# Dense-block gates of a two-layer PEER kernel: one block per layer placed by indirect scatter-add instead of matmul

## The chip, the cores and the metric

The kernel runs on one core of one Trainium2 chip, as one launch. The metric is the device time of one execution in microseconds (us), here the median of three runs. TensorE is called PE (its weight loads PEld), VectorE DVE, ScalarE ACT, GpSimd POOL and SyncE SP. SP issues the plain transfers, POOL the indirect ones; a queue means one engine's instructions, which it takes strictly in the order in which they were compiled.

## The reference

Two layers (DEPTH = 2) work on a latent stream of 512 tokens and a context stream of 256, all of width 1024, in float32. Each layer is a token mixer (a gated recurrence and a short convolution, not touched by the change) and a PEER channel mixer, cut here to what matters:

```python
def peer_ffn(h, wq, subkeys, u, v):
    scores = einsum('bthpd,hpkd->bthpk', (h @ wq)..., subkeys)
    s1, i1 = top_k(scores[..., 0, :], 16)
    s2, i2 = top_k(scores[..., 1, :], 16)
    cand = s1[..., :, None] + s2[..., None, :]
    top, pos = top_k(cand, 16)
    eidx = take_along_axis(i1 * 128 + i2, pos)
    gate = softmax(top)
    act = gelu(einsum('ted,td->te', u[eidx], h))
    return einsum('te,ted->td', gate * act, v[eidx])
```

Every token has 8 heads with 16 experts each out of 128 x 128 = 16,384. A gate is the softmax weight of one (token, expert) pair; an expert that two heads of a token choose gets the sum of both gates.

## The kernel before, in words

The 768 tokens are six blocks of 128: blocks 0 and 1 are the context, 2 to 5 the latents. A layer runs `mixer` and then `peer`. In `peer`, some blocks are **gathered**: for each of the 128 picks of a token, one indirect transfer on POOL (L875) brings 128 rows of 4 KB of U into a tile `gr` or `gs`, DVE multiplies and sums it (L882), and after a gelu the same is done with V (L891). The others are **dense**: all 16,384 experts are computed and multiplied by a gate matrix that is zero where an expert was not picked. In layer 0 blocks 0 and 1 are gathered and 2 to 5 dense (`nt` = 512 tokens). In layer 1 block 5 is gathered, 2 to 4 are dense but for the last 32 tokens of block 4 (`REST`), which are gathered (`nt` = 352).

`peer` goes through four stages:

- **Scores.** `proj` with `wq`, then `top16` and `top_pairs` on DVE.
- **Gates.** `pick` prepares the indices of the first gathered block, and its U gathers start. Then, for each dense block, `select` works out i1, i2 and the gates, and `gates` (L754) turns them into the gate matrix. Per token this is one 128 x 128 float32 matmul of two one-hot matrices (L789, PE); DVE and ACT build the one-hot matrices oA and oB (L773 to L784), ACT copies the result into `stg` (L790), and SP writes 32 tokens at a time, 2 MB, to the DRAM tensor `gd` (L791). Between them, `ahead` computes some of the U products of the dense stage (`experts_in`, a pair of key rows at a time: 48 matmuls, L306 to L308) and writes them to the DRAM tensor `ad`. `AHEAD` = (34, 30) is how many of the 64 pairs each layer makes ahead, and `SPAN` spreads them over the pairs.
- **Dense.** In 16 groups of 4 pairs, `dense` loads the gate tile `gt` from `gd` (L815), takes the U product from `ad` or computes it, multiplies the two on DVE (L823), splits the result in a high and a low part, and multiplies by V (L834 to L836), 192 matmuls a group.
- **Gathers to the end.** The rest of the gathers run on POOL and DVE beside the dense stage. The tile `gs` and the dense tiles take the room of the gate stage's tiles, so they can be used only when that stage is over. The first 96 U gathers of an early block use `gr` alone (three buffers).

The order of each engine's instructions is set at compile time by a scheduler that places them by its own estimate of when each could run; it is fixed in the program. An engine that waits holds up all that stands behind it in its queue. The pieces that the change touches: `setup` (L67), `mixer` (L332), `peer` (L660), `gates` (L754), `dense` (L806) and `arrays_of`. The kernel starts by loading the modulation weights `wmod` (L188), which all later work needs.

Of the kernel before, what the change touches and what calls it, by code (L numbers as in the profile page):

```python
# [19 lines left out]
P = 128  # L20
# [7 lines left out]
PH = 8  # L28
TOPK = 16
# [26 lines left out]
class Kern:  # L56
# [13 lines left out]
    def setup(self):  # L70
# [7 lines left out]
        nc.sync.dma_start(self.ident, a["ident"])  # L78
        cols = c.tile([P, 4], F, name="cols")
        self.ones, self.selc, self.bias = cols[:, 0:1], cols[:, 1:2], cols[:, 2:4]  # L80
# [505 lines left out]


    def top16(self, pool, vals, ixs, src, n):
        nc = self.nc
# [70 lines left out]
    def peer(self, l):  # L660
# [7 lines left out]
        with ExitStack() as es:  # L668
            dr = self.pool(f"dr{l}", stack=es, space=DRAM)
            gd = dr.tile([P // 4, P, nt // 32, 4, 32], F, name="gd")  # L670
            n_ahead = AHEAD[l]
# [15 lines left out]
            with ExitStack() as es2:  # L687
# [33 lines left out]
                def ahead(q):  # L721
                    n = nt // 32
                    for i in range(q * n_ahead // n, (q + 1) * n_ahead // n):
                        A = self.experts_in(l, ap, hx, AHEAD_SET[l][i], nt)
                        nc.sync.dma_start(ad[i], A)

                for k in range(early):
                    self.pick(kp, tbs[gb[k]], 2, *picks[k])
                for n, b in enumerate(db):
                    sel = self.select(kp, tbs[b], 2)  # L730
                    nq = (nt - n * P) // 32
                    self.gates(kp, gd, n, ahead, *sel, min(nq, P // 32))
                    if nq < P // 32:
                        e32 = kp.tile([P, PH * TOPK], I32, name="e32", tag="ri", bufs=1)
                        self.eidx(sel, e32)
                        for j in range(P // r):
                            for dst, src in ((rest[0], e32), (rest[1], sel[2])):
                                nc.sync.dma_start(dst[j * r:(j + 1) * r], src[P - r:, j * r:(j + 1) * r])
            with ExitStack() as es2:
# [13 lines left out]

    def gates(self, kp, gd, n, ahead, i1, i2, gate, nq):  # L754
        nc = self.nc
# [9 lines left out]
        nc.scalar.activation(tn, tg, AF.Copy, scale=-1.0)  # L765
        for q in range(nq):
            stg = kp.tile([P, P, 32], F, name="stg", tag="big", bufs=2)
# [37 lines left out]
    def dense(self, l, es, ap, gd, ad, hx, nt):  # L805
# [147 lines left out]
def arrays_of(x, c, ctx, c_ctx, w_mod, b_mod, norm1_g, norm2_g, w_in, conv_w, w_out,  # L953
# [5 lines left out]
    d = {  # L959
        "ident": np.eye(P, dtype=np.float32),  # L960
        "iota": np.broadcast_to(np.arange(P, dtype=np.float32), (P, P)),
        "masks": np.stack(masks).astype(np.float32).transpose(1, 0, 2),
# [35 lines left out]
```

## Time and profile before

| what | value |
|---|---|
| three runs | 4177.32, 4160.89, 4176.73 us; median 4176.73 us |
| the profiled execution | 4176.49 us, of which the span from first to last instruction is 4174.7 us |
| mean granted PE clock | 0.964 of full speed |
| busy shares | PE 93%, PEld 81%, DVE 81%, ACT 43%, POOL 33% |
| DMA | 1012 MB, mean 242 GB/s |

A line of the profile names the program line (L875), the engine, the operation, out<-in by the tiles' names, and a count; in a timeline it begins with start and duration in us, and the idle time before it stands in brackets with what ended it. "us to landing" is the time from a transfer's issue to its last byte. In a table by stages, each engine has its busy time and its number of instructions, followed by the granted PE clock, the busy share of the 16 DMA engines and what they moved.

### The profile page before, as it was taken

The page shows a single profiled execution, that of the slowest core. Times are in us where ns is not written, and L with a number is a line of the kernel's source. Part 1 is how long each engine was busy: PE and PEld are TensorE (multiplying, and loading weights), DVE is VectorE, ACT ScalarE, POOL GpSimd, SP SyncE. Part 2 cuts the span into 40 slices and gives each one's busy share as a digit, 9 for nine tenths or more (in the row PEclk, how much of TensorE's full clock was granted, in tenths as well). Part 3 has the DMA queues.
Part 4 walks back from the last instruction along what each step waited for, and adds up shares of the span by engine and source line. Part 5 has one row for each costly group of instructions (what it writes and reads, how often), then busy time and mean ns, then how long its engine had stood idle before and what let it go on. Part 6 is the DMA issues. An engine that isn't in the chain of part 4 may idle for free. (4 is left out here: it accounts for less than half of the span.)

```text
span 4174.7 us, 59124 instructions
## 1 busy us (share of the span) xinstructions
PE 3900.6 (93%) x21317; PEld 3371.1 (81%) x21317; DVE 3397.0 (81%) x6491; ACT 1795.4 (43%) x3096; POOL 1396.1 (33%) x1020
## 2 busy tenths in 40 slices
PE   8999999989997999999999989988999669999998
PEld 5888869778886778877777768866899669999998
DVE  4766639989986999888888878758989978999984
ACT  4444332349985232222222245433448943333333
POOL 0211102033331245555555512112023344445430
PEclk8999999999998999999999999989999879999999
DMA  6444122389998899899899921112489989999983
GB/s 223 133 157 157 57 71 87 100 287 323 315 325 273 302 329 361 311 327 331 320 327 322 325 78 56 63 64 85 143 285 334 294 310 355 354 357 354 362 329 111
DMA packets 387717, 1011.97 MB, mean 242 GB/s; under 512 B 31712, under 2 KB 158944, under 8 KB 383072
## 3 DMA queue, kind: packets, MB, share of 16 engines
q1 hardware_dynamic: 267616, 571.94, 39.4%
q0 software_dynamic: 119808, 436.26, 29.4%
q8 instruction: 168, 2.75, 0.3%
q14 instruction: 125, 1.02, 0.1%
HBM read 913.34 MB, written 94.70 MB: 241 GB/s over the span
## 5 line engine op out<-in xcount | busy, mean ns | idle before, releaser
L297 ACT ACTIVATE whi<-wraw 128x1024 fp32r<-128x1024 f32 x624 | 657.4, 1058 | 1238.1 <-PE p L835 517.1
L834 PE MATMUL p<-Wh,whi 128*128 128x512 f32 (+1 forms) x2048 | 726.9, 361 | 60.1 <-ACT Wh L826 47.5
L875 POOL DMA_INDIRECT gr<-in_u,picki x360 | 479.1, 1331 | 877.4 <-DVE gr L882 598.7
L299 DVE TENSOR_TENSOR wlo<-wraw,whi 128x1024 fp32r<-128x1024 f32 x592 | 723.3, 1224 | 59.9 <-ACT whi L297 56.7
L836 PE MATMUL p<-Wh,wlo 128*128 128x512 f32 (+1 forms) x2048 | 733.4, 360 | 12.7 <-DVE wlo L299 11.2
L308 PE MATMUL p<-hxh,wlo 128*128 128x512 f32 (+1 forms) x2048 | 739.4, 362 | 3.4 <-DVE wlo L299 3.3
L835 PE MATMUL p<-Wl,whi 128*128 128x512 f32 (+1 forms) x2048 | 730.7, 359 | 10.5 <-DVE Wl L827 10.3
L306 PE MATMUL p<-hxh,whi 128*128 128x512 f32 (+1 forms) x2048 | 739.4, 361 | 0.5 <-ACT A L802 0.4
L307 PE MATMUL p<-hxl,whi 128*128 128x512 f32 (+1 forms) x2048 | 739.8, 361 | 0.0
L875 POOL DMA_INDIRECT gr<-in_v,picki x312 | 457.0, 1465 | 492.8 <-DVE acc L891 355.6
L882 DVE SCALAR_TENSOR_TENSOR gr<-gr,htok 128x1024 f32<-128x1024 f32 x360 | 436.8, 1221 | 124.3 <-DMA gr<-in_u,picki 123.3
L834 PEld LDWEIGHTS p<-Wh,whi 128*128 128x128 f32 x2048 | 386.5, 190 | 110.9 <-ACT Wh L826 50.1
L836 PEld LDWEIGHTS p<-Wh,wlo 128*128 128x128 f32 x2048 | 386.7, 189 | 65.1 <-DVE wlo L299 25.0
L835 PEld LDWEIGHTS p<-Wl,whi 128*128 128x128 f32 x2048 | 388.2, 190 | 56.8 <-DVE Wl L827 16.3
L891 DVE SCALAR_TENSOR_TENSOR acc<-gr,gw,acc 128x1024 f32<-128x1024 f32 x308 | 394.4, 1281 | 46.2 <-DMA gr<-in_v,picki 44.0
L308 PEld LDWEIGHTS p<-hxh,wlo 128*128 128x128 f32 x2048 | 387.9, 190 | 42.5 <-DVE wlo L299 5.3
L306 PEld LDWEIGHTS p<-hxh,whi 128*128 128x128 f32 x2048 | 388.2, 190 | 38.3 <-ACT A L802 0.8
L307 PEld LDWEIGHTS p<-hxl,whi 128*128 128x128 f32 x2048 | 388.0, 189 | 37.8
L789 PE MATMUL gps<-oA,oB 128*128 128x128 f32 x1728 | 272.2, 300 | 60.7 <-DVE oA L781 31.3
L789 PEld LDWEIGHTS gps<-oA,oB 128*128 128x128 f32 x1728 | 253.8, 209 | 89.1 <-ACT oB L778 43.9
L306 PE MATMUL pj<-h512h,whi 128*128 128x512 f32 x640 | 262.2, 413 | 11.5 <-ACT h512h L367 3.2
L826 ACT ACTIVATE Wh<-A 128x1024 fp32r<-128x1024 f32 (+1 forms) x128 | 118.2, 925 | 334.5 <-DVE A L823 292.4
(320 smaller groups left out, 6696.3 us busy)
## 6 DMA issues: line engine op xcount, KB each, us to landing
wraw<-in_ut SPq DMA_DIRECT2D x256, 512.0 KB, 6.1
wraw<-in_vt SPq DMA_DIRECT2D x256, 512.0 KB, 6.3
gd<-stg SPq DMA_DIRECT2D x27, 2048.0 KB, 14.1
wmod<-in_w_mod SPq DMA_DIRECT2D x96, 512.0 KB, 4.5
wraw<-in_w_in SPq DMA_DIRECT2D x64, 512.0 KB, 3.5
gt<-gd SPq DMA_DIRECT2D x32, 1024.0 KB, 7.9
gt<-gd SPq DMA_DIRECT2D x32, 704.0 KB, 8.9
ad<-A SPq DMA_DIRECT2D x34, 512.0 KB, 7.2
```

Source lines behind the costliest of these rows:

```text
L297: nc.scalar.activation(hi, raw, AF.Copy)
L299: (eng or nc.vector).tensor_tensor(lo, raw, hi.bitcast(F), op=OP.subtract)
L306: nc.tensor.matmul(out, wh[:, k], ah[:, k, :n], start=i == 0, stop=False)
L307: nc.tensor.matmul(out, wh[:, k], al[:, k, :n], start=False, stop=False)
L308: nc.tensor.matmul(out, wl[:, k], ah[:, k, :n], start=False, stop=i == KC - 1)
L789: nc.tensor.matmul(pt[:, s], B[:, s4 + s], A[:, s4 + s], start=True, stop=True)
L834: nc.tensor.matmul(pt, hi[:, j], wh, start=j == 0, stop=False)
L835: nc.tensor.matmul(pt, hi[:, j], wl, start=False, stop=False)
L836: nc.tensor.matmul(pt, lo[:, j], wh, start=False, stop=j == NG - 1)
L875: nc.gpsimd.indirect_dma_start(out=t, out_offset=None, in_=src, in_offset=bass.IndirectOffsetOnAxis(ap=eidx[:, e:e + 1], axis=0))
L882: nc.vector.scalar_tensor_tensor(u, u, 1.0, htok, op0=OP.mult, op1=OP.mult, accum_out=act[:, e:e + 1])
L891: nc.vector.scalar_tensor_tensor(acc, v, w[:, e:e + 1], acc, op0=OP.mult, op1=OP.add)
```

## The change

In each layer the last dense block no longer goes through `gates`. `spread` computes on DVE, for each token and pick, the position of its gate in a DRAM tensor `gs0` or `gs1` (the tiles `gs` of the gathers are something else), and POOL issues 128 indirect transfers per layer; each adds one gate for each of 128 tokens (layer 0) or 96 tokens (layer 1), 4 bytes a token, to what lies there. All 128 write one tensor, so each waits until the one before it has landed. The tensor has to be zero at the start: 7 transfers of 128 x 4096 floats, 2 MB each, copy zeros into it from an input (4 for layer 0, 3 for layer 1). The load of each `gt` is split into a part from `gd` and a part from the new tensor; the second waits for the last scatter. The block for `spread` is selected first. `pick` comes after it in layer 0, and in layer 1 after the gates of the first dense block. `AHEAD` becomes (32, 36).

```diff
-AHEAD = (34, 30)
-SPAN = (34, 60)
+AHEAD = (32, 36)
+SPAN = (32, 60)
+ZCOLS = 4096
...
+            self.spread_begin(l)
             st = self.gla_in(l, 0, wi, hx, hc, hcq)
             for h in range(HEADS):
                 self.gla(l, h, st, lambda: self.gla_gate(h, wi, hx, hcq), last)
+                self.zero_some(l)
...
+    def spread_begin(self, l):
+        nq = (P - REST[l]) // 32
+        row = P * nq * 32
+        self.gs = self.dram.tile([P, row + 256], F, name=f"gs{l}")
+        self.zeros = [(c, min(ZCOLS, row - c)) for c in range(0, row, ZCOLS)]
+
+    def zero_some(self, l):
+        if self.zeros:
+            c, n = self.zeros.pop()
+            self.nc.sync.dma_start(self.gs[:, c:c + n], self.a["zeros"][:, :n])
+
+    def spread(self, kp, sel, nq):
...
+        nc.vector.scalar_tensor_tensor(f, i1, 32.0, f, op0=OP.mult, op1=OP.add)
+        nc.vector.scalar_tensor_tensor(f, i2, float(P * n + 256), f, op0=OP.mult, op1=OP.add)
+        nc.vector.tensor_copy(si, f)
+        nc.vector.tensor_copy(sg, g)
+        for s in range(S):
+            nc.gpsimd.indirect_dma_start(
+                out=self.gs.rearrange("p (x o) -> (p x) o", o=1),
+                out_offset=bass.IndirectOffsetOnAxis(ap=si[:n, s:s + 1], axis=0),
+                in_=sg[:n, s:s + 1], in_offset=None, compute_op=OP.add)
...
-                for k in range(early):
-                    self.pick(kp, tbs[gb[k]], 2, *picks[k])
-                for n, b in enumerate(db):
-                    sel = self.select(kp, tbs[b], 2)
...
+                sel = self.select(kp, tbs[db[-1]], 2)
+                self.spread(kp, sel, (P - r) // 32)
...
+                for n, b in enumerate(db[:-1]):
+                    if n == int(last):
+                        early_picks()
+                    self.gates(kp, gd, n, ahead, *self.select(kp, tbs[b], 2))
...
-                    nc.sync.dma_start(gt.rearrange("p c i t -> p (c i t)"), gd[j // 4].rearrange("p c i t -> p (c i t)"))
+                    nqm = gd.shape[2]
+                    nqs = (nt // 32 - nqm) * P
+                    nc.sync.dma_start(gt[:, :nqm].rearrange("p c i t -> p (c i t)"),
+                                      gd[j // 4].rearrange("p c i t -> p (c i t)"))
+                    nc.sync.dma_start(gt[:, nqm:].rearrange("p c i t -> p (c i t)"),
+                                      self.gs[:, j // 4 * nqs:(j // 4 + 1) * nqs])
```

The compiled order shows where the scheduler put these pieces. Rows that follow one another with the same names stand as one, with their count behind an x.

The first place is SP's queue at the start of the kernel. Before, the 18 loads of `wmod` stand in one row:

```order
L106 DMA resx<-in_x 128x2048 x2
L108 DMA bmod<-in_b_mod 128x96
L110 DMA ng<-in_gains 128x40
L188 DMA wmod<-in_w_mod 128x1024 x18
L124 DMA resc<-in_ctx 128x1024 x2
```

Now, in the same place:

```order
L109 DMA resx<-in_x 128x2048 x2
L111 DMA bmod<-in_b_mod 128x96
L113 DMA ng<-in_gains 128x40
L191 DMA wmod<-in_w_mod 128x1024 x11
L602 DMA gs_466<-in_zeros 128x4096 x4
L602 DMA gs_19789<-in_zeros 128x4096 x3
L191 DMA wmod<-in_w_mod 128x1024 x7
L127 DMA resc<-in_ctx 128x1024 x2
```

The zero copies of both layers stand ahead of the last 7 of those 18 loads, although the code writes them in the mixers.

The second place is POOL's queue at the end of the scatters, in the changed program (before, it holds gathers alone). In layer 0 (`gs_466` is the DRAM tensor of layer 0):

```order
L924 DMA gr<-in_u,picki_5047 128x1024
L924 DMA gr<-in_v,picki_5047 128x1024
L622 DMA gs_466<-sg,si 2129920x1
L924 DMA gr<-in_v,picki_5047 128x1024 x2
L622 DMA gs_466<-sg,si 2129920x1 x49
L924 DMA gs<-in_u,picki_5047 128x1024 x8
```

In layer 1 (`gs_19789`):

```order
L622 DMA gs_19789<-sg,si 1605632x1
L924 DMA gr<-in_u,picki_22648 128x1024 x2
L622 DMA gs_19789<-sg,si 1605632x1
L924 DMA gr<-in_u,picki_22648 128x1024
L924 DMA gr<-in_v,picki_22648 128x1024
L622 DMA gs_19789<-sg,si 1605632x1
L924 DMA gr<-in_v,picki_22648 128x1024 x2
L622 DMA gs_19789<-sg,si 1605632x1 x37
L924 DMA gs<-in_u,picki_22648 128x1024 x8
```

The first 11 scatters of layer 0 and the first 31 of layer 1 stand ahead of the first gather; then scatters and gathers alternate, as in the first rows here; 49 and 37 stand at the end, with no gather among them.

The third place is DVE's queue between the last gates of layer 1 and the first product of the dense stage. Before:

```order
L773 TENSOR_TENSOR oB<-gt_27006,iota 128x384
L781 TENSOR_SCALAR oA<-iota,gt_27002,gt_27010 128x128 x3
L784 TENSOR_TENSOR oA<-gt_27002,iota 128x640
L882 SCALAR_TENSOR_TENSOR gr,act<-gr,htok 128x1024 x10
L823 TENSOR_TENSOR A<-A,gt 128x704 x2
```

Now:

```order
L817 TENSOR_TENSOR oB<-gt_26169,iota 128x384
L825 TENSOR_SCALAR oA<-iota,gt_26165,gt_26173 128x128 x3
L828 TENSOR_TENSOR oA<-gt_26165,iota 128x640
L931 SCALAR_TENSOR_TENSOR gr,act<-gr,htok 128x1024 x2
L302 TENSOR_TENSOR wlo<-wraw,whi 128x1024
L931 SCALAR_TENSOR_TENSOR gr,act<-gr,htok 128x1024
L302 TENSOR_TENSOR wlo<-wraw,whi 128x1024
L931 SCALAR_TENSOR_TENSOR gr,act<-gr,htok 128x1024 x75
L872 TENSOR_TENSOR A<-A,gt 128x704 x2
```

Between the last gate and the first product, DVE now takes 78 gathered tiles where it took 10; in layer 0 it takes 24 where it took none.

## Rows read from the trace of the kernel before

**Rows 1.** Page: span, busy time and share of each engine.

```profile
span 4174.7 us, 59124 instructions
PE 3900.6 (93%) x21317; PEld 3371.1 (81%) x21317; DVE 3397.0 (81%) x6491; ACT 1795.4 (43%) x3096; POOL 1396.1 (33%) x1020
```

**Rows 2.** Busy times by stage; columns in the second line.

```profile
core 0: us, PE busy (x) PEld busy (x) DVE busy (x) ACT busy (x) POOL busy (x), PEclk, DMA share, GB/s
0.00:40.00 40.00, 28.10 (x192) 14.07 (x192) 8.36 (x46) 11.96 (x25) 1.97 (x9) 0.79 0.96 367
834.00:1294.00 460.00, 434.61 (x2360) 371.97 (x2358) 398.30 (x755) 370.37 (x861) 159.47 (x124) 0.98 0.92 309
1294.00:1330.00 36.00, 18.14 (x66) 14.97 (x67) 14.45 (x32) 11.70 (x24) 0.94 (x1) 0.59 0.86 295
1330.00:2400.00 1070.00, 1030.30 (x4456) 837.55 (x4455) 945.62 (x1190) 291.13 (x284) 554.39 (x384) 0.99 0.91 323
3051.00:3361.00 310.00, 267.25 (x1657) 254.54 (x1657) 279.30 (x527) 251.20 (x599) 108.42 (x87) 0.92 0.91 310
3361.00:3391.00 30.00, 4.52 (x25) 4.33 (x24) 14.82 (x25) 4.47 (x9) 11.04 (x11) 0.56 0.91 317
3391.00:4100.00 709.00, 704.29 (x4316) 693.50 (x4317) 638.87 (x728) 251.28 (x270) 319.02 (x222) 1.00 0.93 342
```

**Rows 3.** Timeline of SP's DMA queue, first 25 us: start, duration, issue.

```profile
start us, us, engine line op out<-in xcount [idle before <-releaser]
...
3.76 19.59 SPq L188 DMA_DIRECT2D wmod<-in_w_mod  x18
24.25 1.61 SPq L124 DMA_DIRECT2D resc<-in_ctx  x2
```

**Rows 4.** Timeline of PE, first 45 us, three of its rows.

```profile
25.56 1.08 PE L190 MATMUL pmod<-wmod,cond 128*32 128x256 f32 x8 [0.45 <-DMA wmod<-in_w_mod]
...
28.04 1.08 PE L190 MATMUL pmod<-wmod,cond 128*32 128x256 f32 x8 [1.39 <-DMA wmod<-in_w_mod]
...
42.26 0.80 PE L306 MATMUL pj<-h512h,whi 128*128 128x512 f32 x1 [2.39 <-ACT whi L297]
```

**Rows 5.** Gate tile stg: DMA line of the page, landing over all.

```profile
gd<-stg SPq DMA_DIRECT2D x27, 2048.0 KB, 14.1
...
DMA to landing us min/median/max: 9.4/14.1/18.0
```

**Rows 6.** Page, groups: gate matmul of one token, as two instructions each.

```profile
L789 PE MATMUL gps<-oA,oB 128*128 128x128 f32 x1728 | 272.2, 300 | 60.7 <-DVE oA L781 31.3
```

**Rows 7.** Gather tile gr: issue on POOL, use on DVE, landing.

```profile
engine op xcount: duration ns min/median/max, first and last start us, forms
L875 POOL DMA_INDIRECT gr<-in_u,picki x360: 932/1147/3557, 834.8 to 3951.2; - x180
L882 DVE SCALAR_TENSOR_TENSOR gr<-gr,htok x360: 1168/1220/1298, 839.8 to 3961.4; 128x1024 f32<-128x1024 f32 x180
...
DMA to landing us min/median/max: 4.2/7.2/12.4
```

**Rows 8.** Score tile sd, 64 to 128 KB written by SP's queue.

```profile
DMA to landing us min/median/max: 1.5/1.8/7.9
```

**Rows 9.** Timeline of POOL: first gathers of layer 0 and of layer 1.

```profile
834.76 1.41 POOL L875 DMA_INDIRECT gr<-in_u,picki  x1 [96.79 <-DVE picki L843]
836.48 0.94 POOL L875 DMA_INDIRECT gr<-in_u,picki  x1 [0.30 <-issue]
...
3051.34 1.30 POOL L875 DMA_INDIRECT gr<-in_u,picki  x1 [117.36 <-DVE picki L843]
```

**Rows 10.** Timeline of DVE: last gate and first product, layer 0.

```profile
1293.77 0.82 DVE L784 TENSOR_TENSOR oA<-gt,iota 128x640 f32<-128x640 f32 x1
1316.10 2.36 DVE L823 TENSOR_TENSOR A<-A,gt 128x1024 f32<-128x1024 f32 x2 [21.51 <-DMA gt<-gd]
```

**Rows 11.** Timeline of PE: first V product, layer 0, layer 1.

```profile
1318.52 1.65 PE L834 MATMUL p<-Wh,whi 128*128 128x512 f32 x3 [17.60 <-ACT Wh L826]
...
3391.20 1.25 PE L834 MATMUL p<-Wh,whi 128*128 128x352 f32 x3 [25.67 <-ACT Wh L826]
```

**Rows 12.** Timeline of DVE: end of the gates and gathers after, layer 1.

```profile
3361.30 0.82 DVE L784 TENSOR_TENSOR oA<-gt,iota 128x640 f32<-128x640 f32 x1
...
3368.76 1.23 DVE L882 SCALAR_TENSOR_TENSOR gr<-gr,htok 128x1024 f32<-128x1024 f32 x1 [3.20 <-DMA gr<-in_u,picki]
...
3372.14 1.23 DVE L882 SCALAR_TENSOR_TENSOR gr<-gr,htok 128x1024 f32<-128x1024 f32 x1 [2.15 <-DMA gr<-in_u,picki]
...
3384.24 1.23 DVE L882 SCALAR_TENSOR_TENSOR gr<-gr,htok 128x1024 f32<-128x1024 f32 x1 [0.44 <-DMA gr<-in_u,picki]
```

**Rows 13.** Page, DMA issues: gate loads of the dense stage.

```profile
gt<-gd SPq DMA_DIRECT2D x32, 1024.0 KB, 7.9
gt<-gd SPq DMA_DIRECT2D x32, 704.0 KB, 8.9
```

More of the change, by code (lines that the diff above doesn't have):

```diff
@@ L78, in setup @@
         nc.sync.dma_start(self.ident, a["ident"])
-        cols = c.tile([P, 4], F, name="cols")
+        cols = c.tile([P, 5], F, name="cols")
+        self.tcol = cols[:, 4:5]
+        nc.sync.dma_start(self.tcol, a["tcol"])
         self.ones, self.selc, self.bias = cols[:, 0:1], cols[:, 1:2], cols[:, 2:4]
@@ L585, in conv @@
             nc.vector.tensor_tensor(self.oc.at(4 + j, sl.start, sl.stop), o[:, sl], src, op=OP.mult)
+    def spread_begin(self, l):
[8 more added lines that the diff above has]
+    def spread(self, kp, sel, nq):
+        nc = self.nc
+        i1, i2, g = sel
+        S = PH * TOPK
+        n = nq * 32
+        a = kp.tile([P, S], U32, name="sa", tag="ri", bufs=1)
+        f = kp.tile([P, S], F, name="sf", tag="tail", bufs=1)
+        si = kp.tile([P, S], I32, name="si", tag="si", bufs=1)
+        sg = kp.tile([P, S], F, name="sg", tag="sg", bufs=1)
+        nc.vector.tensor_copy(a, i1)
+        nc.vector.tensor_scalar(a, a, 2, None, op0=OP.logical_shift_right)
+        nc.vector.tensor_copy(f, a)
+        nc.vector.tensor_scalar(f, f, float((nq - 1) * P), self.tcol, op0=OP.mult, op1=OP.add)
+        nc.vector.scalar_tensor_tensor(f, i1, 32.0, f, op0=OP.mult, op1=OP.add)
[7 more added lines that the diff above has]
+                in_=sg[:n, s:s + 1], in_offset=None, compute_op=OP.add)
     def top16(self, pool, vals, ixs, src, n):
@@ L669, in peer @@
             dr = self.pool(f"dr{l}", stack=es, space=DRAM)
-            gd = dr.tile([P // 4, P, nt // 32, 4, 32], F, name="gd")
+            nqm = (len(db) - 1) * (P // 32)
+            gd = dr.tile([P // 4, P, nqm, 4, 32], F, name="gd")
             n_ahead = AHEAD[l]
@@ L721, in ahead @@
                 def ahead(q):
-                    n = nt // 32
+                    n = nqm
                     for i in range(q * n_ahead // n, (q + 1) * n_ahead // n):
@@ L725, in ahead, with early_picks @@
                         nc.sync.dma_start(ad[i], A)
-                for k in range(early):
-                    self.pick(kp, tbs[gb[k]], 2, *picks[k])
-                for n, b in enumerate(db):
-                    sel = self.select(kp, tbs[b], 2)
[L731 to L738, printed above, removed]
+                def early_picks():
+                    for k in range(early):
+                        self.pick(kp, tbs[gb[k]], 2, *picks[k])
+                sel = self.select(kp, tbs[db[-1]], 2)
+                self.spread(kp, sel, (P - r) // 32)
+                if r:
+                    e32 = kp.tile([P, PH * TOPK], I32, name="e32", tag="ri", bufs=1)
+                    self.eidx(sel, e32)
+                    for j in range(P // r):
+                        for dst, src in ((rest[0], e32), (rest[1], sel[2])):
+                            nc.sync.dma_start(dst[j * r:(j + 1) * r], src[P - r:, j * r:(j + 1) * r])
+                for n, b in enumerate(db[:-1]):
+                    if n == int(last):
+                        early_picks()
+                    self.gates(kp, gd, n, ahead, *self.select(kp, tbs[b], 2))
             with ExitStack() as es2:
@@ L752, in peer, with gates @@
                         nc.sync.dma_start(self.xd[:, c], self.res.x[:, c])
-    def gates(self, kp, gd, n, ahead, i1, i2, gate, nq):
+    def gates(self, kp, gd, n, ahead, i1, i2, gate):
         nc = self.nc
@@ L765, in gates @@
         nc.scalar.activation(tn, tg, AF.Copy, scale=-1.0)
-        for q in range(nq):
+        for q in range(P // 32):
             stg = kp.tile([P, P, 32], F, name="stg", tag="big", bufs=2)
@@ L960, in arrays_of @@
         "ident": np.eye(P, dtype=np.float32),
+        "tcol": ((np.arange(P) >> 5) * P + (np.arange(P) & 31)).astype(np.float32)[:, None],
+        "zeros": np.zeros((P, ZCOLS), np.float32),
         "iota": np.broadcast_to(np.arange(P, dtype=np.float32), (P, P)),
```

## The prediction

> **What bounds the kernel now.** The page [rows 1] puts PE at 93% of the span and DVE at 81%, but an average over stages hides what each stage waits for, so the table by stages comes next [rows 2]. The first 40 us belong to the DMA engines (busy 0.96, 367 GB/s): PE waits there for `wmod` loads [rows 4]. In the gate stage of layer 0 (834 to 1294) PE is busy 435 of 460 us, in that of layer 1 (3051 to 3361) 267 of 310, with DVE at 279; PE and DVE are both nearly full. The dense stages are PE's: 1030 of 1070 us and 704 of 709. Between gates and dense stand two short gaps, 24.5 us in layer 0 from the last gate on DVE to the first V product on PE [rows 10, 11] and 30 in layer 1 [rows 11, 12], in which PE has nothing else to do.
>
> So a microsecond taken from PE's gate work counts where PE sets the pace, and a microsecond between the last gate and the first V product counts in full: the dense stage cannot start without `gt`, and every group needs it.
>
> **What the change takes away.** A token's gate costs PE two instructions, 272.2 us for 1728 of them [rows 6], so 0.315 us a token: 128 tokens make 40 us in layer 0, 96 make 30 in layer 1. A pair of U products is 48 matmuls. The dense rows give 1070 us for 4456 instructions, 0.240 each, so 11.5 us a pair in layer 0, and 709 us for 4316, 0.164 each, so 7.9 in layer 1 [rows 2]. Two pairs more in layer 0's dense stage are +23 us there and as much less in its gate stage; six fewer in layer 1's are -47 there and +47 before. The gates' work on DVE and ACT falls too, which lets PE set the pace; the eight small DVE operations of `spread` are nothing beside it. By PE alone the last gate would fall at 1294 - 40 - 23 = 1231 in layer 0. In layer 1 PE's work becomes 267 - 30 + 47 = 284 us, so 3051 + 284 = 3335.
>
> **What it adds: the zero copies.** They are 7 x 2.1 MB = 14.7 MB, placed among the loads for which PE waits at the start; SP issues 18 of these between 3.8 and 23.4 us [rows 3]. What stands behind the copies is late by their duration, and nothing else is there for PE: its first projection starts at 42 us [rows 4], after the last of them. No row shows a copy from DRAM to DRAM. Below, the start moves 367 GB/s at a busy share of 0.96, so 382 at full: 38 us. Above, 2 MB written to `gd` take 14.1 us at the median, 99 us for seven. I take the quickest such write, 9.4 us [rows 5], because the start has no other writes: **66 us**.
>
> **The scatters, step by step.** Each waits for the one before, so a step is a full round: the pause between two POOL transfers (0.30 us [rows 9]), the issue and the landing. No row shows a 4-byte accumulate. The nearest is the gather, the same kind of transfer with 128 rows: 4.2 us at the quickest, 7.2 at the median [rows 7]. It moves 0.52 MB, 1.4 us at 382 GB/s, so without the bytes 2.8 us in quiet and 5.8 among other traffic. A step is 3.1 us in quiet, **6.1** in the gate stage, where the DMA engines are 0.91 busy [rows 2]. Bounds: below, 0.30 and the shortest issue 0.93 with the quickest landing of a small write, 1.5 [rows 8], 2.7 us; above, the median gather with its bytes, 7.5 us, everywhere.
>
> By the Trainium skill ("DMA: Bandwidth & Descriptors", section "Anatomy of one DMA — SWDGE (gpsimd) path") a transfer issued by POOL has a fixed cost of about 2.0 us, whatever its size. With it a quiet step would be an estimated 2.3 us and the time 69 us shorter than the sum below; no row of this trace shows a small indirect transfer that could decide.
>
> **Until the last gate.** The scatters can start when the first selection is done, about where the first gather starts now: 835 and 3051 [rows 9]. DVE's order takes 96 gathers before the last gate in layer 0 and 42 in layer 1. POOL can be three buffers ahead, so 68 and 53 scatters stand before that point in its queue. At 6.1 us they end at 835 + 415 = 1250 and 3051 + 323 = 3374. Both are later than PE's 1231 and 3335, and DVE cannot pass the gathers, so I take 1250 and 3374.
>
> **After the last gate.** Here is the main term. DVE still has 24 gathers in layer 0 and 78 in layer 1 ahead of the first product. POOL has 11 and 38 scatters among them, and then 49 and 37 alone. A gather with nothing else to do costs 2.58 us (six intervals from 3368.76 to 3384.24 [rows 12]), and a scatter between two gathers at least its issue and pause, 1.24 us. Layer 0: 24 x 2.58 + 11 x 1.24 = 76 us, 49 x 3.1 = 152, and 10 for the quarter of a gate load that is left (the whole lands in 7.9 us [rows 13]), the product and the split. The first V product is at 1250 + 76 + 152 + 10 = 1488 instead of 1318.5: +170, and with the two pairs **+193**. Layer 1: 78 x 2.58 + 38 x 1.24 = 248 us, 37 x 3.1 = 115, 10: 3374 + 373 = 3747 instead of 3391, +356, less 47 for the six pairs: **+309**. During this SP stands at the load of the first `gt`, with all later weights behind it, and PE's next instruction is a V product: nothing covers the wait. The gathers done early relieve DVE in the dense stage, where PE is full (704 of 709 us [rows 2]), so that gives nothing back.
>
> **The sum.** 66 + 193 + 309 = 568 us on the profiled execution's 4176.5, which is the median of the runs to 0.3 us: **4745 us**. The writes of `gd` fall by as many bytes as the zeros bring; no stage waits for them.
>
> **The rivals.**
>
> *Short steps.* Every bound low: 38 us at the start, the last gates at PE's 1231 and 3335, a gather at DVE's own 1.3 us with the scatters between hidden, 2.7 us a step. Layer 0: 1231 + 31 + 132 + 10 = 1404, +86, with the pairs +109. Layer 1: 3335 + 101 + 100 + 10 = 3546, +155, less 47, +108. Sum +255: 4432 us. For it speaks that DMA is quiet when SP stands; against it, that gathers with little else beside them took 2.58 us.
>
> *Long steps.* An accumulate lands like a median gather, 7.5 us a step, 99 us at the start. Layer 0: 835 + 510 + 62 + 83 + 368 + 10 = 1868, +549, with the pairs +572. Layer 1: 3051 + 398 + 201 + 285 + 278 + 10 = 4223, +832, less 47, +785. Sum +1456: 5633 us. For it speaks that 4 bytes must be read, added and written back; against it, the quick small writes.
>
> *The chain is hidden: faster.* If all 128 scatters land before the last gate, the gaps after it stay as now. Layer 0 gains 40 us, layer 1 its last gate 26 us earlier and 47 us of pairs: -113, with the 66 of the start 4130 us. This needs a step of (1231 - 835) / 128 = 3.1 us in layer 0 and (3335 - 3051) / 128 = 2.2 in layer 1, among full DMA traffic, and a chip that does not keep the order of POOL's and DVE's queues. For it speaks that POOL is busy only 159 of 460 us [rows 2]; against it, that order.
>
> **How the numbers follow.** The forecast has 0.68, short steps 0.12, long steps 0.15, the hidden chain 0.04, and a stop halfway to it, near no change, 0.01. A half per cent is about what a measurement of this kernel can tell from no change. So slower has 0.95, faster 0.04, the same 0.01. The range runs from 4480, in the upper part of short steps, to 5100, a loaded step of 6.1 us also in the quiet stretches (86 x 3.0 = 258 us more) with half of the 33 us by which the zeros may be dearer, and something for gathers that wait behind scatters.
>
> **What would show each step.** In the changed profile: the seven copies keep the DMA engines busy for 66 us and PE's first projection starts near 108 us; 256 scatters at 2.8 us to landing where nothing else runs, POOL idle before most of them for the last one's landing; PE idle for about 240 us between the last gate and the first V product of layer 0 and 370 us in layer 1, SP waiting at `gt`; dense stages as long as now but for the pairs; PE's share near 81%. The prediction is wrong if the V products follow the gates within 50 us, if a quiet step is under 2 us or over 5, or if the start is not late.

## The result and the profile after

The changed kernel takes 4767.78 us (median of 6 runs, 4759.2 to 4777.78), the kernel before 4177.02 beside it: a ratio of 1.1431, interval 1.1412 to 1.145. That is slower by 591 us; the prediction said 4745, range 4480 to 5100. The profiled execution has a span of 4757.4 us, 582.7 more than before. The forecast case came about, with terms that were off in both directions.

The page of the changed kernel: first the busy times of the whole, then three of the lines in 40 slices, then two groups. PE falls from 93% to 81% [rows 1], although its busy time is only 59 us less (3900.6 before).

```profile
PE 3841.3 (81%) x20863; PEld 3312.0 (70%) x20863; DVE 3355.9 (71%) x6367; ACT 1669.7 (35%) x2750; POOL 1827.4 (38%) x1276
...
PE   4999999889820799999999899889785005999998
DVE  2766659778730799888888688489676414999974
POOL 0211111355664244565566122120456753444410
...
L883 PE MATMUL p<-Wh,whi 128*128 128x512 f32 (+1 forms) x2048 | 725.7, 361 | 585.1 <-ACT Wh L875 563.4
...
L622 POOL DMA_INDIRECT gs<-sg,si x256 | 442.0, 1727 | 629.1 <-DMA gs<-sg,si 388.0
```

The holes in the PE line, at slices 12 to 14 and 31 to 34, are the stretches between the gates and the dense stage of each layer. The group L622 is the scatters: 442 us of POOL's own work, and 388 us in which POOL waited for the scatter before. The group L883 is the first V product of each sum: PE waited 585 us ahead of it.

The table by stages, to be held against [rows 2]: start; mixer 0; gates 0; the rest of the early gathers; the last scatters; dense 0; mixer 1; gates 1; gathers and last scatters; dense 1.

```profile
core 0: us, PE busy (x) PEld busy (x) DVE busy (x) ACT busy (x) POOL busy (x), PEclk, DMA share, GB/s
0.00:85.00 85.00, 29.45 (x192) 14.69 (x192) 10.22 (x50) 13.21 (x27) 1.97 (x9) 0.62 0.97 348
85.00:878.00 793.00, 762.77 (x4861) 632.01 (x4862) 557.80 (x1762) 305.46 (x548) 121.12 (x87) 0.98 0.34 111
878.00:1329.00 451.00, 381.96 (x1945) 324.05 (x1944) 333.05 (x620) 290.99 (x664) 262.41 (x168) 0.92 0.83 253
1329.00:1404.00 75.00, 15.69 (x77) 12.87 (x75) 34.34 (x53) 7.19 (x10) 50.58 (x36) 0.62 0.89 274
1404.00:1572.00 168.00, 0.35 (x1) 0.35 (x2) 2.77 (x3) 1.43 (x2) 76.76 (x50) 0.50 0.17 17
1572.00:2640.00 1068.00, 1033.07 (x4479) 838.83 (x4479) 952.08 (x1212) 292.64 (x285) 559.78 (x387) 0.99 0.91 325
2640.00:3290.00 650.00, 586.06 (x2974) 485.04 (x2973) 483.02 (x1351) 266.18 (x442) 118.66 (x94) 0.94 0.25 82
3290.00:3640.00 350.00, 294.61 (x1917) 291.92 (x1915) 256.08 (x466) 229.61 (x490) 157.08 (x102) 0.91 0.73 231
3640.00:3960.00 320.00, 0.00 (x0) 0.00 (x0) 94.60 (x152) 1.67 (x2) 202.46 (x150) 0.50 0.52 142
3960.00:4757.00 797.00, 737.34 (x4424) 712.21 (x4424) 631.90 (x706) 261.33 (x285) 276.54 (x196) 0.98 0.80 292
```

In the rows from 1329 to 1572 and from 3640 to 3960 PE does 16 us of work in 563. From 1404 to 1572 hardly an engine works but POOL, and that for 77 of 168 us, and the DMA engines move 17 GB/s.

**Start.** SP's DMA queue and PE, where [rows 3, 4] show the same places before:

```profile
4.38 10.22 SPq L191 DMA_DIRECT2D wmod<-in_w_mod  x11
15.56 8.18 SPq L602 DMA_DIRECT2D gs<-in_zeros  x7
24.56 37.69 SPq L191 DMA_DIRECT2D wmod<-in_w_mod  x7
```

```profile
69.52 1.08 PE L193 MATMUL pmod<-wmod,cond 128*32 128x256 f32 x8 [42.94 <-DMA wmod<-in_w_mod]
...
85.48 0.80 PE L309 MATMUL pj<-h512h,whi 128*128 128x512 f32 x1 [1.98 <-ACT whi L300]
```

The copies stand between 11 and 7 loads of `wmod`, and PE waits 42.94 us for a load behind them. Its first projection starts at 85.5 us instead of 42.3: +43 us for the 14.7 MB of the copies, 340 GB/s.

**Scatters.** POOL's timeline in the gate stage of layer 0, where two gathers stand among the scatters, and in the run of 49 at the end:

```profile
1053.48 3.21 POOL L622 DMA_INDIRECT gs<-sg,si  x1 [1.81 <-DMA gs<-sg,si]
1057.00 1.12 POOL L924 DMA_INDIRECT gr<-in_u,picki  x1 [0.30 <-issue]
1062.00 1.58 POOL L622 DMA_INDIRECT gs<-sg,si  x1 [3.88 <-DMA gs<-sg,si]
1063.88 0.97 POOL L924 DMA_INDIRECT gr<-in_u,picki  x1 [0.30 <-DVE ix L688]
1065.15 0.94 POOL L924 DMA_INDIRECT gr<-in_u,picki  x1 [0.30 <-issue]
1068.79 1.60 POOL L622 DMA_INDIRECT gs<-sg,si  x1 [2.70 <-DMA gs<-sg,si]
...
1555.72 1.54 POOL L622 DMA_INDIRECT gs<-sg,si  x1 [1.69 <-DMA gs<-sg,si]
1559.00 1.55 POOL L622 DMA_INDIRECT gs<-sg,si  x1 [1.74 <-DMA gs<-sg,si]
1562.34 1.55 POOL L622 DMA_INDIRECT gs<-sg,si  x1 [1.78 <-DMA gs<-sg,si]
```

Here (the two stretches are parted by the dots) a scatter comes mostly every 4.5 to 9 us among gathers, and every 3.3 us alone: 1.55 us of POOL's own work and 1.74 us until the one before has landed. From 1408.38 to 1562.34 there are 47 steps, 3.28 us each; the 36 steps of the run in layer 1 (from 3838.93) take 3.16.

**Behind the gates.** The first products of the dense stage on DVE and the first V products on PE ([rows 10, 11] show 1316.10, 1318.52 and 3391.20 before), and SP's wait:

```profile
1569.23 2.36 DVE L872 TENSOR_TENSOR A<-A,gt 128x1024 f32<-128x1024 f32 x2 [166.82 <-issue]
...
3959.62 1.69 DVE L872 TENSOR_TENSOR A<-A,gt 128x704 f32<-128x704 f32 x2 [122.21 <-DMA gt<-gs]
```

```profile
1571.65 1.65 PE L883 MATMUL p<-Wh,whi 128*128 128x512 f32 x3 [226.96 <-ACT Wh L875]
...
3961.44 1.25 PE L883 MATMUL p<-Wh,whi 128*128 128x352 f32 x3 [325.57 <-ACT Wh L875]
```

```profile
engine line waited for: us in total, times, longest us
SPq L863 <- DMA gs<-sg,si: 202.4, 1, 202.4
```

In layer 0 SP stood 202.4 us at the first load from the scatters' tensor (the `gs` of this line), with all weights behind it. PE waited 226.96 us in layer 0 and 325.57 in layer 1.

### The profile page after: what moved, and what is told of

Read it like the earlier page. It is cut to its first block, busy times and chain, and to the rows that moved or that the text cites. A ratio compares the mean times of both kernels' runs of the same rounds, so it can differ in the third digit from the quotient of the medians.

```text
span 4757.4 us, 58144 instructions
## 1 busy us (share of the span) xinstructions
PE 3841.3 (81%) x20863; PEld 3312.0 (70%) x20863; DVE 3355.9 (71%) x6367; ACT 1669.7 (35%) x2750; POOL 1827.4 (38%) x1276
## 5 line engine op out<-in xcount | busy, mean ns | idle before, releaser
L883 PE MATMUL p<-Wh,whi 128*128 128x512 f32 (+1 forms) x2048 | 725.7, 361 | 585.1 <-ACT Wh L875 563.4
L300 ACT ACTIVATE whi<-wraw 128x1024 fp32r<-128x1024 f32 x624 | 656.3, 1057 | 1233.6 <-PE p L884 504.9
L883 PEld LDWEIGHTS p<-Wh,whi 128*128 128x128 f32 x2048 | 385.9, 190 | 639.1 <-ACT Wh L875 568.3
L622 POOL DMA_INDIRECT gs<-sg,si x256 | 442.0, 1727 | 629.1 <-DMA gs<-sg,si 388.0
L872 DVE TENSOR_TENSOR A<-A,gt 128x1024 f32<-128x1024 f32 (+1 forms) x128 | 133.7, 1052 | 297.8 <-issue 166.8
```

Of the source, the lines that this page charges most:

```text
L300: nc.scalar.activation(hi, raw, AF.Copy)
L622: nc.gpsimd.indirect_dma_start(out=self.gs.rearrange("p (x o) -> (p x) o", o=1), out_offset=bass.IndirectOffsetOnAxis(ap=si[:n, s:s + 1], ...
L883: nc.tensor.matmul(pt, hi[:, j], wh, start=j == 0, stop=False)
```

## The experiments

The theory that went into them: the changed kernel loses its time to (a) a chain of 128 scatters a layer, each of which waits for the landing of the one before, which ends long after the last gate, and (b) the zero copies at the start. The rivals: (c) the order alone, which puts 24 and 78 gathers behind the last gate; (d) the scatters' own work on POOL rather than their waits; (e) the other numbers of U pairs made ahead; (f) the addition in memory.

All kernels are the changed one with one edit, unless said otherwise. The runs of the kernel before that stood beside them had medians from 4174.67 to 4177.45 us, so the times are compared directly with 4768 us. The table divides each profiled span at seven starts: the first projection on PE, DVE's last gate (oA, L781 before, L825 after; some of the edits shift the line) in each layer, the first and the last V product of each layer.

| kernel | time | start | gates 0 | gap 0 | dense 0 | mixer, gates 1 | gap 1 | dense 1 | end |
|---|---|---|---|---|---|---|---|---|---|
| before | 4177 | 42 | 1251 | 25 | 1087 | 956 | 30 | 759 | 24 |
| changed | 4768 | 85 | 1243 | 243 | 1105 | 952 | 332 | 771 | 25 |
| zeros late | 4730 | 42 | 1238 | 242 | 1103 | 963 | 336 | 770 | 24 |
| no scatter | 4187 | 86 | 1179 | 43 | 1117 | 902 | 35 | 773 | 51 |
| half the scatters | 4317 | 86 | 1241 | 42 | 1112 | 960 | 80 | 766 | 24 |
| four tensors | 4404 | 87 | 1284 | 47 | 1117 | 997 | 35 | 770 | 60 |
| pairs of before | 4771 | 86 | 1255 | 242 | 1094 | 934 | 344 | 792 | 24 |
| alternate, zeros late | 4665 | 42 | 1294 | 166 | 1108 | 955 | 310 | 773 | 24 |
| no early gathers | 4884 | 86 | 1125 | 209 | 1139 | 1057 | 272 | 774 | 217 |
| plain copy | 4657 | 86 | 1220 | 195 | 1117 | 941 | 296 | 774 | 25 |
| no scatter, zeros late | 4146 | 42 | 1188 | 43 | 1111 | 895 | 36 | 778 | 50 |
| the same, pairs of before | 4141 | 42 | 1186 | 51 | 1096 | 893 | 30 | 784 | 63 |
| before, new pairs | 4221 | 42 | 1242 | 23 | 1111 | 963 | 29 | 774 | 24 |

### The zero copies placed in the mixers

```diff
-            nc.sync.dma_start(raw, src)
+            self.wdma = nc.sync.dma_start(raw, src).ins
...
+            with self.tc.issue_after(self.wdma):
                 self.nc.sync.dma_start(self.gs[:, c:c + n], self.a["zeros"][:, :n])
```

> Edit: each zero copy is queued on SP behind a weight load of the head it was written for, so that it runs inside the mixers and not at the start; nothing else. Theory (the copies are 43 us at the start, and nothing anywhere else): the first projection on TensorE is back at 42 to 50 us (85.5 in the changed kernel), every later marker is that much earlier, and the time is 4725 us (4712 to 4738). Rival (the 14.7 MB cost their bandwidth wherever they run): the mixers grow by what the start gives back, and the time stays within 10 us of 4768.

4729.6 us (ratio to before 1.1326, 1.1295 to 1.1358): 38 us less. The first projection is back at 41.9 us, the gain is in the column of the start, and the mixers pay little for it (5 us less in the column of layer 0, 11 more in that of layer 1); the DMA engines had room there, 0.34 busy in the second row of the table by stages. (b) holds, with 38 to 43 us.

### No scatter, half of them, and a chain in four parts

```diff
-        for s in range(S):
+        for s in range(0):            # no scatter
+        for s in range(0, S, 2):      # half
...
-                out=self.gs.rearrange("p (x o) -> (p x) o", o=1),
+                out=self.gss[s % 4].rearrange("p (x o) -> (p x) o", o=1),   # four tensors
```

> Edit: none of the 128 scatter steps of a layer is issued; the zero copies, the indices and the loads stay. Left out: the gates of the spread block, whose products are then zero. Theory (the chain of scatters is the whole loss but for the copies): the first V product follows the last gate by under 40 us in both layers (237 and 325 us in the changed kernel), which takes off about 200 + 290 us; the time is 4270 us (4220 to 4310). Rival (gathers were put behind the gates by the order of the program and cost as much without any scatter): the gap in the second layer stays over 150 us and the time is over 4400 us.

> Edit: every second of the 128 steps of a layer is issued (64). Left out: the other half of the spread block's gates. Theory (a chain at about 3.2 us a step when nothing lies between, slower when gathers do): the run of scatters alone at the end is gone in both layers (161 us and 117 us); of the gathers behind the last gate 10 are left of 24 and 27 of 78, at 2.6 us each and as many us again for the scatters among them. First layer gap about 50 us, second about 120 us; the time is 4370 us (4310 to 4440), so that halving the steps gives back more than half of what leaving all out gives. Rival (the loss is in proportion to the number of scatters): halfway between the changed kernel and the kernel without scatters, about 4520 us.

> Edit: scatter number s goes to tensor s mod 4 in place of one tensor; all 128 steps of a layer are issued as before, each waits only for the one four before it. Left out: three quarters of the spread block's gates, which land in tensors that nothing reads. Theory (the step is long because each scatter waits until the one before it has landed): POOL issues them one behind the other, at 1.55 us of its own and 0.3 us to issue, 1.85 to 2.2 us a step where no gather lies between; all 128 are out before the last gate in the first layer, and the gap is under 40 us there and under 60 us in the second; the time is 4290 us (4230 to 4350), near the kernel without scatters. Rival (the step is POOL's own work or the transfers' traffic, not the wait): the steps stay over 3 us and the time over 4600 us.

Without scatters the time is 4187.1 us (ratio 1.0021, 1.0008 to 1.0034): the scatters cost 581 us, all of the loss but 10 us (the 43 us of the copies are still in this time, and the shorter gate stages make up for most of them). That is 33 us under the expected range, because the gate stages became shorter too (1243 to 1179 us in layer 0, and 952 to 902 in the column of layer 1). The gaps are down to 43 and 35 us, from 243 and 332; the scheduler now puts 9 and 8 gathers behind the last gate, not 24 and 78. So the order of (c) came with the scatters. What that order would cost with no scatter in it, no run shows, since the scheduler orders each of these programs anew.

Half the scatters: 4316.86 us (1.0333, 1.0303 to 1.0363). It gives back 451 of the 581 us, more than three quarters, where proportion would give 290. Gap 0 is 42 us (50 expected), gap 1 80 (120 expected). The gaps alone are 453 us shorter than in the changed kernel (201 and 252): what costs most is how far the chain reaches beyond the gates. The gate stage of layer 0 is as long with half the scatters (1241 us) as with all (1243, where 68 of the 128 stand ahead of the last gate).

Four tensors: 4403.92 us (1.0547, 1.0517 to 1.0577), 54 us above the top of what was expected. The wait for the landing is gone as expected. POOL at the start of layer 0's scatters:

```profile
929.33 1.54 POOL L623 DMA_INDIRECT gs<-sg,si  x1 [0.30 <-issue]
931.17 1.55 POOL L623 DMA_INDIRECT gs<-sg,si  x1 [0.30 <-issue]
933.03 0.98 POOL L925 DMA_INDIRECT gr<-in_u,picki  x1 [0.30 <-issue]
```

A step is 1.85 us, 1.54 of work and the pause of 0.30; the last of the 128 starts at 1225.5 us, long before the last gate, and the gaps are 47 and 35 us. So 364 us of the loss (4768 - 4404) go with the waits, (a). But the gate stages are longer than without scatters, by 104 us and 94 us, and longer even than in the changed kernel, by 41 and 45. DVE's waits in the gate stage of layer 0, first the kernel without scatters (878 to 1266), then with four tensors (881 to 1370), then the changed kernel (878 to 1329); the columns are the total, the number of waits and the longest:

```profile
DVE gr L931 <- DMA gr<-in_u,picki: 46.3, 24, 4.9
```

```profile
DVE gr L932 <- DMA gr<-in_u,picki: 165.6, 50, 27.3
```

```profile
DVE gr L931 <- DMA gr<-in_u,picki: 115.4, 40, 19.3
```

DVE takes gates and gathered rows in a fixed order. Where 26 scatters stand ahead of the first gather and more among the gathers, the gathers are late, DVE waits for them (46 us without scatters, 166 with), and the gates behind them in DVE's order wait too. The 120 us more of these waits fit the 104 us by which the stage is longer. So the remaining 217 us (4404 - 4187) are in the main (d): 256 scatters of 1.85 us on POOL (1.72 in layer 1), 457 us of which just under half comes through. The expectation did not count this second cost.

### A gather for every scatter, and no gathers at all

In the cut, `self.steps` holds the layer's 128 scatters; the copies are moved as in the first experiment.

```diff
+            with ExitStack() as es:      # alternate: gather e behind scatter e
+                if self.steps:
+                    es.enter_context(self.tc.issue_after(self.steps.pop(0)))
                 u = fetch(a[f"u{l}"], e, n0)
...
-EARLY = (1, 1)
+EARLY = (0, 0)                        # no early gathers
```

> Edit: gather e of the early block is queued on POOL behind scatter e, so that the two alternate one to one in place of two gathers to a scatter, and the zero copies are queued inside the mixers. Nothing is left out. Theory (the waits of the chain can hold a gather, 1.3 us in a wait of 1.7 us, so that the runs of 49 and 37 scatters alone need not be): a pair takes 3.5 to 5 us; the runs alone at the end are gone; the first V product comes about 150 us earlier in each layer than with late zeros alone (4730 us); the time is 4430 us (4330 to 4550). Rival (gathers wait for VectorE, which waits in its order for the gates, and a scatter behind such a gather waits with it, so that what leaves the end comes back in the middle): 4650 us or more.

> Edit: no block's picks are made early (EARLY 0 in both layers), so that no gather stands among the gates and the 128 scatters have POOL to themselves there; the 120 gathers of a layer go to its dense stage. Nothing is left out. Theory (scatters and gathers hold each other up on POOL, and VectorE's gates stand behind the gathers in order): the chain takes 128 steps of 3.2 us, 410 us, and ends in the first layer with the gates, near 1300 us on the clock of the changed kernel, the first V product within 40 us of the last gate (237 before); in the second layer the chain outlasts the gates by 120 to 170 us in place of 325; the dense stages take 50 to 100 us (first) and 170 to 200 us (second) more for the gathers that moved there; the time is 4640 us (4560 to 4730). Rival (the chain is no faster without gathers, as its steps wait for the landing alone): the gaps stay and the time is over 4950 us.

Alternating gives 4665.07 us (1.1169, 1.115 to 1.1187), 65 us less than late zeros alone and 115 above the expected range; the run of 49 is gone, but the chain still takes 652 us in layer 0 (837.6 to 1489.8), 5.1 us a step, and the gates end 57 us later than with late zeros alone. The rival stated there (what leaves the end comes back in the middle) came about for most of it.

Without gathers among the scatters the time is 4883.96 us (1.1702, 1.168 to 1.1724), between theory (4640) and rival (over 4950). The reason is in POOL's timeline of this kernel, first beside the gates, then after them:

```profile
1102.89 2.18 POOL L622 DMA_INDIRECT gs<-sg,si  x1 [1.80 <-DMA gs<-sg,si]
1107.72 1.54 POOL L622 DMA_INDIRECT gs<-sg,si  x1 [2.65 <-DMA gs<-sg,si]
...
1377.24 1.55 POOL L622 DMA_INDIRECT gs<-sg,si  x1 [1.67 <-DMA gs<-sg,si]
1380.53 1.54 POOL L622 DMA_INDIRECT gs<-sg,si  x1 [1.74 <-DMA gs<-sg,si]
```

Even alone on POOL, a step beside the gates' other traffic is 4.83 us (853.4 to 1215.7, 75 steps, DMA engines 0.6 busy), in quiet 3.30 (1235.15 to 1396.9, 49 steps). My estimate used the quiet step throughout: 410 us for the chain, where it took 544. At 4.83 us, 128 steps are 618 us, and the gates of this kernel end 357 us after the first scatter (853.4 to 1210.5): putting the scatters first on POOL does not let them end with the gates. The 1125 us of the gate column show the other side: with no gathers in DVE's order the gates end 118 us earlier than in the changed kernel. The gathers, though, do not fit into the dense stages, where I had put them: those of layer 0 are still being issued at 2792 us, 234 us behind its last V product (105 us more in the column of layer 1's mixer), and the end takes 217 us instead of 25.

### Writing without adding

```diff
-                in_=sg[:n, s:s + 1], in_offset=None, compute_op=OP.add)
+                in_=sg[:n, s:s + 1], in_offset=None)
```

> Edit: the scatters write in place of adding; all steps, their order and their waits stay. Left out: the sum where two heads of a token chose the same expert (the later value stands). Theory (a step is POOL's instruction and the way of a small transfer until its landing is seen; the addition is nothing of it): the steps in the runs alone stay at 3.1 to 3.3 us and the time within 25 us of 4768. Rival (reading the target, adding and writing is what makes a step long): the step falls to 2.6 us or less and the time by 100 us or more.

4657.34 us (1.1154, 1.1127 to 1.1181), 110 us less: the theory falls and the numbers of the rival are met, so (f) is a part of the loss. The run at the end of layer 0 in this kernel:

```profile
1487.08 0.96 POOL L622 DMA_INDIRECT gs<-sg,si  x1 [1.43 <-DMA gs<-sg,si]
1489.47 0.96 POOL L622 DMA_INDIRECT gs<-sg,si  x1 [1.43 <-DMA gs<-sg,si]
```

A step is 2.39 us here, 0.96 of work and 1.43 of waiting, against 1.55 and 1.74; the last 35 steps take 2.44 us each, against 3.27. The addition costs about 0.85 us a step, some two thirds of it on POOL. Most of the chain stays.

### The U pairs made ahead

```diff
-AHEAD = (32, 36)          # pairs of before, in the changed kernel
-SPAN = (32, 60)
+AHEAD = (34, 30)
+SPAN = (34, 60)
...
-AHEAD = (34, 30)          # new pairs, in the kernel before
-SPAN = (34, 60)
+AHEAD = (32, 36)
+SPAN = (32, 60)
```

> Edit: the numbers of U pairs made ahead are those of the kernel before (34 and 30 in place of 32 and 36). Theory (the first layer's dense stage pays for two pairs, the second's is held by VectorE and not by TensorE, so that pairs are worth nothing there, and the pairs made ahead lie in a stage that waits anyway): 18 us less in the first layer's dense stage (1106 to 1088 us), no change in the second's (771 us); the time is 4750 us (4735 to 4765). Rival (six pairs are worth 7.9 us each in the second dense stage, as the prediction has it): 18 us less and 47 us more, 4797 us (4785 to 4810).

> Edit: the kernel before with 32 and 36 pairs of U products made ahead in place of 34 and 30; no scatter, no copy. Theory (a pair made ahead moves its TensorE time from the dense stage to the gate stage of its layer; the first layer's dense stage gains 12 to 23 us and the second's loses about 20, as VectorE and its order hold it before TensorE does, while the gate stages change the other way): 4180 us (4165 to 4200). Rival (six pairs are worth 47 us in the second dense stage and are hidden in its gate stage): 4150 us or less.

In the changed kernel the old numbers give 4770.74 us (1.1428, 1.14 to 1.1456): no difference. In layer 0's dense stage two pairs are worth 12 us, in layer 1's six are worth 21, and the other columns take it back. I expected a gain of 18; (e) is out. In the kernel before, the new numbers cost 44 us (4221.07; 1.0116, 1.0093 to 1.0138), which neither theory (4180) nor rival (4150) had: in the profiled execution, which is 34 us longer, dense 0 grows by 24 us, as two pairs should make it, dense 1 by 15, although it has six pairs less to compute, and the other columns change by no more than 9. So the pairs are a loss in the kernel before and nothing in the changed one.

### What it would be worth if the scatters were free

Two kernels without scatters and with the copies in the mixers, the second also with 34 and 30 pairs.

> Edit: no scatter step is issued and the zero copies are queued inside the mixers: what the change would come to if placing the spread block's gates cost nothing. Left out: the gates of the spread block, whose products are then zero. Theory (the copies cost 38 to 43 us wherever nothing else of the change is in the way, and the gates taken off TensorE shorten the gate stages as forecast): 4187 less 40, 4147 us (4135 to 4160), 0.7% under the kernel before, and this is the most that the change could give. Rival (without scatters the start of the first layer is covered by something else): 4175 us or more, nothing to gain at all.

> Edit: as the kernel without scatter steps and with late zero copies, and with the numbers of pairs of the kernel before (34 and 30). Left out: the gates of the spread block, whose products are then zero. Theory (the pairs cost 44 us in the kernel before, from 4177 to 4221, and the same where no scatter stands in the gate stage): 4146 less 44, 4102 us (4090 to 4120), which is what placing one block's gates for nothing would be worth alone, the 70 us that its matmuls take in the gate stages. Rival (the pairs do not matter once the gates leave TensorE, as they do not in the changed kernel, 4771 against 4768 us): 4146 us within 12.

4145.77 us (0.9934, 0.9915 to 0.9953) and 4140.83 us (0.9919, 0.9904 to 0.9933): 31 to 34 us under the kernel before, and the pairs make no difference here (the rival of the second holds). As the scheduler orders these two programs, this is what the change gives when placing the block costs nothing. The second kernel shows why it is no more. Its gate columns are 128 us shorter than before (65 and 63), and 99 us come back: 26 in gap 0, 9 in dense 0, 25 in dense 1, 39 at the end. The last stretches of it (first dense stage 1, last the end):

```profile
core 0: us, PE busy (x) PEld busy (x) DVE busy (x) ACT busy (x) POOL busy (x), PEclk, DMA share, GB/s
3398.00:3998.00 600.00, 575.50 (x3526) 565.47 (x3524) 528.87 (x600) 205.19 (x221) 272.30 (x188) 1.00 0.93 337
3998.00:4082.00 84.00, 81.71 (x503) 80.33 (x502) 74.61 (x91) 25.69 (x29) 40.59 (x32) 1.00 0.88 308
4082.00:4146.00 64.00, 18.50 (x51) 7.40 (x50) 30.02 (x39) 8.61 (x13) 17.75 (x14) 0.61 0.46 158
```

After the last V product PE is busy 18.5 of 64 us and DVE still has gathered rows to add: POOL's last V gather starts at 4106.58 us, where in the kernel before the last one starts at 4047.98, 102 us ahead of the last V product. So with fewer gates on PE the gathers and DVE set the end.

No version that does all of the scatters' work was found that beats the kernel before; the best is alternation with late copies, 4665 us. Pairs of before, four tensors and late copies were not put together with a kernel that sums the four tensors, since four tensors without the sum and its loads already cost 4404 us.

## Why the prediction was right

By its own steps, on the profiled spans (568 forecast, 582.7 found):

- **Zero copies, +66.** Mis-sized: +43. They ran at 340 GB/s, which is near the lower bound of 38 us; a write of one gate tile was the wrong row to take. Moved away, they give 38 us back.
- **Gates of layer 0 end at 1250 on the old clock.** Mis-sized by 35 us: 1328.3 less the 43 of the start is 1285. The first 11 scatters went at 4.2 us, but the 58 steps behind them, among gathers, took 7.05 (920.22 to 1329.0), not 6.1. Those 58 steps hold 99 gathers, which the forecast put at nothing: of the 7.05 us about 3.9 are the scatter's own (2.1 on POOL, 1.8 of waiting) and 3.1 the gathers' with their waits. That the scatters and not PE set this end was right: without them the gates end at 1265.4 less 43.7, 1222, against the 1231 that PE alone was given. That it is their rounds is not shown: with the chain cut in four the last scatter starts at 1225.5, and the gates end at 1370.
- **From the last gate to the first V product, layer 0: 238 us.** 243 found. 24 gathers and 11 scatters took 76 us (1328.3 to 1403.9), as forecast; the run of 49 took 158 to its last start (1562.34) where 152 were forecast, since a quiet step is 3.28 us and not 3.1; 9 us passed from there to the first V product, forecast 10.
- **Gates of layer 1, 13 us later.** Found: 3 us earlier, counted from the last V product of layer 0.
- **From the last gate to the first V product, layer 1: 373 us.** 332 found. 78 gathers and 38 scatters took 209 us, not 248: counting 2.58 and 1.24 us one behind the other was too much. A gather between scatters probably lies in part in a scatter's wait; no run shows it by itself. The run of 37 took 114 to its last start (3838.9 to 3952.7) and 9 from there, forecast 115 and 10.
- **Two pairs more in dense 0, +23.** +18 found.
- **Six pairs fewer in dense 1, -47.** This step failed, in sign: +12. The prediction took each microsecond of U products off PE as one off the stage, because PE was busy 704 of 709 us [rows 2], and passed over DVE's share beside it. Over the whole stage PE's busy time fell only from 754 to 728 us, and its idle time rose from 5 to 43. The middle of the stage, first before, then in the changed kernel, columns as in the table by stages, each with PE's longest waits around it (3420 to 4050 and 4020 to 4550; total, number, longest):

```profile
3650.00:3750.00 100.00, 99.81 (x615) 98.66 (x614) 92.92 (x94) 34.78 (x37) 48.37 (x34) 1.00 0.96 357
PE p L836 <- DVE wlo L299: 1.5, 1, 1.5
...
4220.00:4320.00 100.00, 91.39 (x548) 87.26 (x548) 91.69 (x93) 33.21 (x36) 47.29 (x35) 1.00 0.95 355
PE p L885 <- DVE wlo L302: 12.1, 12, 1.5
PE p L884 <- DVE Wl L876: 10.2, 11, 3.4
```

DVE is about as busy as before (93 and 92 of 100 us), and PE now waits for it. The kernel before with 36 pairs shows the same without any scatter: 774 us instead of 759, and 34 us in which PE waits for DVE behind the first product. In the changed kernel with the pairs of before the stage takes 792 us: so there the six pairs do give back 21 us, and the rest of the change makes the stage 33 us longer. What in the rest does that was not tried, and stays open.

The errors sum to +15 us (-23, +35, +5, -16, -41, -5, +59, +1). The mechanism is borne out: the two gaps grew by 520 us (218 and 302), where 556 were forecast. That the total came within 15 us is luck: the 59 us of dense 1 and the 41 of the gap ahead of it cancel for the most part, as do the first two terms.

The estimate beside the sum, from the Trainium skill ("DMA: Bandwidth & Descriptors", section "Anatomy of one DMA — SWDGE (gpsimd) path"), a fixed cost of about 2.0 us and so a quiet step of 2.3 us: the plain copy's 2.39 us agree with it, the adding scatter's 3.28 do not, so the measured round decides; between the two lies the addition.

Of the rivals, *short steps* and *long steps* were ruled out by the quiet step, 3.28 us where they had 2.7 and 7.5. The *hidden chain*, 4130 us with its copies, is nearest to the kernel without scatters, 4187. Dense 1 makes more than the difference of 57: 773 us, 14 more than before, where this rival has 47 less; the other terms partly cancel it. The order of POOL's and DVE's queues, which spoke against this rival, is a part of what prevents it. The loaded step is the other: with no gather on POOL it is 4.83 us, where 3.1 were needed. Of the forecast's marks, PE's share of 81% and the idle stretch of layer 0 (227 us, forecast about 240) were met, that of layer 1 was 326 instead of 370; the first projection was to start near 108 us and started at 85.5; the landing of 2.8 us is not shown by the trace, which has only the step.

## What to carry to other kernels

Price a chain of dependent small transfers by its full round (issue, landing, and the load of the stage in which it runs: here 3.3 us in quiet, 4.8 beside traffic, 7 with the gathers in between) and set count times round against the time until its result is needed, before counting what it saves elsewhere. Look then at what else goes through the same queue and who takes its results in a fixed order: cutting the chain in four removed the waits and left 217 us, in the main because the gathers behind the scatters were late for a VectorE that had to take them ahead of the gates. And before moving work off an engine, leave it out altogether and time that: here that gave no more than 34 us of 4177, since of 128 us saved in the gate stages 99 came back in the stages behind them.

## What the runs showed of the hardware

- An indirect transfer of 128 rows of 4 bytes with addition occupies POOL for 1.55 us, without addition for 0.96, nearly what a gather of 128 rows of 4 KB takes at the least (0.93 us [rows 7]). A round in quiet is 3.28 and 2.39 us. The 0.59 us on POOL were not expected.
- With 96 rows instead of 128 (layer 1) the steps are little shorter: 1.42 us on POOL with addition and 0.91 without, and 3.16 us a round with addition.
- Transfers that do not wait for each other follow at 1.85 us where no gather lies between, POOL's work and the same pause of 0.30 us as between gathers [rows 9].
- Copies from DRAM to DRAM ran at 340 GB/s by the delay that they caused, and at 345 GB/s from 24 to 62 us, where the changed kernel moves hardly anything else and the DMA engines are full (share 1.00). The loads at the start of the kernel before move 367 [rows 2].
